# Loading the result rows of an expert layer ahead of a data-dependent loop, and another split of the adds between VectorE and TensorE

## The chip, the cores and the metric

The kernel runs on one core of a Trainium2 chip. The core has five engines, each with an instruction queue of its own: TensorE (PE, matmuls), VectorE (DVE), ScalarE (ACT), GpSimd (POOL) and SyncE (SP, which here only issues transfers); 16 DMA engines move data between the chip's memory (HBM) and the on-chip memory (SBUF). TensorE writes to a small memory of its own, PSUM. The metric is the device time of one execution in microseconds; lower is better.

## What is computed

The reference is one decoder layer on 1024 tokens of width 1024, all in float32: a mixer (gated DeltaNet and dilated attention), a layer norm, a mixture of experts, a second layer norm. The edit lies at the end, in the experts' sum and the second norm. Each token goes to two of 32 experts, and their two results are added, each with its gate:

```python
def grouped_expert_mlp(xf, expert_ids, gates, w_gate, w_up, w_down):
    ...
    def expert_block(args):
        xb, e = args
        hid = jax.nn.silu(xb @ w_gate[e]) * (xb @ w_up[e])
        return hid @ w_down[e]
    ys = lax.map(expert_block, (xs, blk_expert)).reshape(n_slots, d)
    y = jnp.zeros((t + 1, d), F32).at[slot_tok].add(ys.astype(F32) * slot_gate[:, None])
    return y[:t]

# in reference(), at the end of the layer
y = hierarchical_moe(h, w_router_group[l], ...)
x = layer_norm(DEEPNORM_ALPHA * x + (1 + gate2) * y, ln2_g[l], ln2_b[l])
```

## The kernel before, in words

**The experts.** The kernel handles a fixed number of 81 blocks of 32 rows (`SEQ`, `ORDER`), each of one expert. For a block, TensorE transposes the gathered rows (`px`), multiplies them with the expert's gate and up weights (`ph`), and with its down weights (`po`); VectorE scales the result into `yo` (L1378, `block_d`), and GpSimd scatters `yo` by an indirect DMA into `y2d` in HBM (L1329, `scatter_y`), which has one row of 1024 for each token and choice, 2048 rows in all. The weights stand in SBUF in four buffers for gate and up (`wgu0` to `wgu3`, 4 MB each) and three for down (`wd0` to `wd2`, 2 MB each), handed out in turn; `fgu` and `fd` are the lists of free ones. When the last weights are loaded, the next free `wgu` buffer takes the residual stream `x1d` (`xall`, L1486), and the next free `wd` buffer the scale and offset of the norm (`lnb`, L1490).

**The loop for surplus rows.** The fixed blocks hold so many rows for each expert. If more rows come for one, `overflow()` (L1431) handles the surplus in a loop whose count `nov` is read from data on the chip; for the inputs used here the count is zero, and the loop is passed. All engines hold the loop's branch. On either way past it, through the loop or around it, each engine waits until every semaphore that was in use has the value it has at the loop's end; the semaphores named DMAHW belong to transfers that SyncE or ScalarE issued, DMASW to those of GpSimd.

**The final stage.** Two free `wgu` buffers, `yall[0]` and `yall[1]`, take the rows of `y2d`: eight loads on SyncE's queue (L1511), one for each tile of 128 tokens, of 2 x 128 rows of 4 KB. `combine(t)` adds for one tile the two result rows and the residual row, and takes the row sums. It does so in one of three ways, chosen by two tuples of tile numbers: tiles in `DADD` are added on VectorE (L1517), and VectorE adds the residual and sums (L1530, `tensor_tensor_reduce`); tiles in `ASUM` are added on TensorE by matmuls with the identity, all three parts, and ScalarE copies and sums (L1528); for the rest TensorE adds the two result rows, and VectorE adds the residual and sums. Then ScalarE takes the sum of squares (L1533). `norm(t)` computes the reciprocal root with a power function on GpSimd (`rsqrt`, L448), applies scale and offset in two VectorE passes (L1540, L1541), and SyncE stores the tile (L1542). The tiles are written one behind the other, `combine(t)` ahead of `norm(t - 1)`; a scheduler sets the order in each engine's queue from that.

Of the kernel before, what the change touches and what calls it, by code (L numbers as in the profile page):

```python
# [20 lines left out]
P = 128  # L21
D = 1024
S = 1024
NT = S // P
# [99 lines left out]
def build(nc, tc, I, out):  # L124
    V, A, G, T, SY = nc.vector, nc.scalar, nc.gpsimd, nc.tensor, nc.sync

    def mm(o, l, r, start=True, stop=True):
        return T.matmul(o, l, r, start=start, stop=stop)  # L128
# [3 lines left out]
    with es:  # L132
# [17 lines left out]
        y2d = nc.dram_tensor("y2d", [2 * S, D], F32)[:, :]  # L150
# [1170 lines left out]
        def gather_x(pool, idx):  # L1321
            xg = pool.tile([P, 256], F32, name="xg", bufs=XB)
            G.indirect_dma_start(out=xg, out_offset=None, in_=h2v,  # L1323
                                 in_offset=bass.IndirectOffsetOnAxis(ap=idx, axis=0),
                                 bounds_check=4 * S - 1, oob_is_err=False)
            return xg
# [15 lines left out]
        def block_x(pool, psp, xg):  # L1342
            px = psp.tile([P, 2, P], F32, name="px", bufs=2)
            for hh in range(2):
                pe(T.transpose(px[:, hh, :], xg[:, hh * P:(hh + 1) * P], ident))  # L1345
            xT = pool.tile([P, 2, P], F32, name="xT", bufs=3)
            A.copy(xT, px)  # L1347
            return xT

        def block_gu(pool, psp, xT, wgu):  # L1350
            wgu = wgu.rearrange("p (k c x) -> p k c x", k=KD, c=4)
            ph = psp.tile([P, 2, P], F32, name="ph", bufs=2)
            for k in range(KD):
                q, hh = divmod(k, 2)
                for c_ in range(4):
                    pe(mm(ph[32 * c_:32 * c_ + 32], xT[:, hh, 32 * q:32 * q + 32], wgu[:, k, c_],
                          start=(k == 0), stop=(k == KD - 1)))
            th = pool.tile([P, P], F32, name="th", bufs=2)
            A.activation(th, ph[:, 0], AF.Silu)  # L1359
            V.tensor_tensor(th, th, ph[:, 1], op=OP.mult)  # L1360
            return th

        def block_h(pool, psp, th):
            pt = psp.tile([P, P], F32, name="pt", bufs=2)
            pe(T.transpose(pt, th, ident))  # L1365
            hT = pool.tile([P, P], F32, name="hT", bufs=2)
            V.tensor_copy(hT, pt)  # L1367
            return hT

        def block_d(pool, psp, hT, gcol, wd, b_, idx):  # L1370
            wd = wd.rearrange("p (c d) -> p c d", c=4)
            po = psp.tile([P, 256], F32, name="po", bufs=2)
            for c_ in range(4):
                for n_ in range(4):
                    pe(mm(po[32 * n_:32 * n_ + 32], hT[:, 32 * c_:32 * c_ + 32], wd[:, c_, n_ * 256:(n_ + 1) * 256],
                          start=(c_ == 0), stop=(c_ == 3)))
            yo = pool.tile([P, 256], F32, name="yo", bufs=YB)
            V.scalar_tensor_tensor(yo, po, gcol, g2t, op0=OP.mult, op1=OP.mult)  # L1378
            scatter_y(b_, idx, yo)
# [14 lines left out]
        fgu, fd = list(range(NA, 4)), list(range(NA, 3))  # L1394
# [9 lines left out]
        def ring(slot):  # L1404
            return wpools["wgu%d" % slot].tile([P, 2 * KD * FF], F32, name="wgu%d" % slot)

        def ring_d(slot):
            return wpools["wd%d" % slot].tile([P, 4 * D], F32, name="wd%d" % slot)
# [8 lines left out]
        def bx(n):  # L1417
            if n < nb:
                xTs[n] = block_x(xp_, pm_, xgs.pop(n))

        def down(n):
            i, b_ = blocks[n]
            block_d(xp_, pm_, hTs.pop(n), gat[:, b_:b_ + 1], wts[i][1], b_, sct[:, b_:b_ + 1])
            if last[i] == n:
                fd.append(slots[i][1])
# [5 lines left out]
        def overflow():  # L1431
            chain[0] = None
            with tc.For_i(0, nov, 1):
                bh = xp_.tile([P, N2], F32, name="bh", bufs=1)
                V.tensor_scalar(bh, bf_[:, 0], ctr, None, op0=OP.is_equal)
                pc_ = pm_.tile([P, 2], F32, name="px", bufs=2)
                for i in range(2):
                    for q in range(4):
                        for a_ in range(N2):
                            mm(pc_[32 * q:32 * q + 32, i:i + 1], Th[:, i, a_, :], bh[:, a_:a_ + 1],  # L1440
                               start=(a_ == 0), stop=(a_ == N2 - 1))
                ic = xp_.tile([P, 4], I32, name="ic", bufs=1)
                gcl = xp_.tile([P, 4], F32, name="gcl", bufs=1)
                V.tensor_scalar(ic[:, 0:1], pc_[:, 0:1], K["pcol"][:, 1:2], None, op0=OP.add)
                V.tensor_scalar(ic[:, 1:2], ic[:, 0:1], ~(4 * S), None, op0=OP.bitwise_and)
                V.tensor_copy(gcl[:, 0:1], pc_[:, 1:2])
                V.tensor_scalar(gcl[:, 1:2], ctr, float(-NB), None, op0=OP.add)
                el = xp_.tile([P, NE], F32, name="el", bufs=1)
                V.tensor_scalar(el, oend, gcl[:, 1:2], None, op0=OP.is_le)
                V.tensor_reduce(gcl[:, 2:3], el, AX.X, OP.add)  # L1450
                V.scalar_tensor_tensor(ic[:, 2:3], gcl[:, 2:3], 128.0, K["pcol"][:, 0:1], op0=OP.mult, op1=OP.add)
                wgu, wd = ring(fgu[0]), ring_d(fd[0])
                for w_, v_ in ((wgu, wgv), (wd, wdv)):
                    G.indirect_dma_start(out=w_, out_offset=None, in_=v_,
                                         in_offset=bass.IndirectOffsetOnAxis(ap=ic[:, 2:3], axis=0))
                xT = block_x(xp_, pm_, gather_x(xp_, ic[:, 1:2]))
                block_d(xp_, pm_, block_h(xp_, pm_, block_gu(xp_, pm_, xT, wgu)), gcl[:, 0:1], wd, NB, ic[:, 0:1])
                chain[0] = None
                V.tensor_scalar(ctr, ctr, 1.0, None, op0=OP.add)

        ctr = rtk.tile([P, 1], F32, name="ctr")
        V.memset(ctr, float(NB))
# [10 lines left out]
        for n, (i, b_) in enumerate(blocks):  # L1473
# [23 lines left out]
            hTs[n] = block_h(xp_, pm_, th)  # L1497
            bx(n + 2)
        down(nb - 1)
        overflow()  # L1500
        xes.close()

# [1 line left out]
        fps = ExitStack()  # L1504
        fp = fps.enter_context(tc.tile_pool(name="fp", bufs=1, reuse_waits="tile"))
        pf_ = fps.enter_context(tc.tile_pool(name="pf_", bufs=1, space=PSUM))
        yall = [ring(fgu[j]).rearrange("p (t k d) -> p t k d", t=4, k=2) for j in range(2)]
        DADD, ASUM = (0, 4), (1, 3, 5, 7)
        y2r = y2d.rearrange("(k t p) d -> t p k d", k=2, p=P)
        for t in range(NT):  # L1510
            SY.dma_start(yall[t // 4][:, t % 4], y2r[t])  # L1511

        def combine(t):
            ya, yb = (yall[t // 4][:, t % 4, k] for k in range(2))
# [84 lines left out]
```

## Time and profile before

| what | us |
|---|---|
| median of 3 runs (1355.63 to 1357.18) | 1357.07 |
| the profiled execution's own time | 1359.02 |
| its span, first to last instruction | 1357.2 |
| TensorE busy (89% of the span) | 1201.2 |
| VectorE busy (45%) | 616.0 |
| ScalarE busy (25%) | 335.1 |
| GpSimd busy (30%) | 409.3 |

The rows further down come from this one profiled execution. Times are microseconds from the start of the span. A row of the timeline is the start, the duration, the engine, the source line, the operation with its tiles, how many such followed each other, and in brackets how long the engine was idle ahead of it and what ended that. DVE is VectorE, and names that end in q are an engine's sequencer: what it does there (issuing transfers, waiting on semaphores, branching) is no busy time. An idle engine costs nothing where another one, or a transfer, sets the end.

### The profile page before, as it was taken

To read this page: it belongs to the slowest core of one execution; us is meant where nothing else is said; L and a number is where in the kernel's file an instruction comes from. 1 tells how busy PE (TensorE), PEld (TensorE's weight loads), DVE (VectorE), ACT (ScalarE), POOL (GpSimd) and SP (SyncE) were. 2 spreads that over 40 slices of the span, in tenths; PEclk is the share of its full clock that TensorE was granted. 3 is DMA by queue.
4 is the path that set the end of the run, shared out by engine and by line. 5 is a ranking of instruction groups with operands and counts; after the bars stand their busy time and mean duration, and the time that the engine had idled before them with its cause. 6 is when DMAs were issued, how large, how long until landed. Compare 5 with 4: busy or idle time off the path is not lost.

```text
span 1357.2 us, 32321 instructions
## 1 busy us (share of the span) xinstructions
PE 1201.2 (89%) x13901; PEld 813.3 (60%) x13901; DVE 616.0 (45%) x1404; ACT 335.1 (25%) x757; POOL 409.3 (30%) x396
## 2 busy tenths in 40 slices
PE   4898999999997989999988459999699999999956
PEld 0476777868785766867766335555355555555522
DVE  0859385674626747577987731111011111111126
ACT  1654343333322333344211101011011111111003
POOL 0223242332223404131532433333233333333113
PEclk8899999999998989999988659999899999999978
DMA  9210001110114335344436859999999999999965
GB/s 378 98 32 33 33 32 34 47 34 17 48 48 134 129 120 162 121 173 110 138 120 250 354 206 420 425 424 423 428 424 411 374 424 422 424 421 423 409 250 220
DMA packets 50629, 311.13 MB, mean 229 GB/s; under 512 B 10226, under 2 KB 18148, under 8 KB 40756
## 3 DMA queue, kind: packets, MB, share of 16 engines
q1 hardware_dynamic: 36064, 282.60, 52.1%
q0 software_dynamic: 8928, 21.00, 4.1%
q10 hardware_dynamic: 5492, 5.44, 1.2%
q8 instruction: 111, 1.82, 0.5%
q14 instruction: 34, 0.28, 0.1%
HBM read 286.56 MB, written 26.89 MB: 231 GB/s over the span
## 4 chain that ended last, share of the span: by engine, by line
PE 40%; DMA 11%; DVE 10%; issue 4%; POOL 3%; ACT 1%; POOLq 0%; SPq 0%; ACTq 0%; DVEq 0%
PE ph L128 17%; PE po L128 9%; DMA wd<-in_k_wd 8%; PE pj L128 5%; DMA araw<-in_w_ada 2%; PE pc L128 2%; PE pg L128 2%; PE pt L1365 1%; DVE acc L259 1%; PE px L1345 1%; POOL wlo L243 1%; DVE oh L1020 1%; DMA y2d<-yo,sct 1%; PE pg L787 1%; ACT sq L1533 1%
## 5 line engine op out<-in xcount | busy, mean ns | idle before, releaser
L128 PE MATMUL ph<-wgu,xT 128*32 128x256 f32 x5184 | 299.0, 383 | 0.0
L128 PEld LDWEIGHTS ph<-wgu,xT 128*32 128x32 f32 x5184 | 160.3, 110 | 113.7 <-issue 16.3
L128 PE MATMUL pj<-hhi,whi 128*128 128x512 f32 x448 | 193.5, 432 | 5.7 <-ACT akq L500 2.4
L128 PE MATMUL pj<-hlo,whi 128*128 128x512 f32 x448 | 181.5, 405 | 3.1 <-DVE hlo L234 2.9
L128 PE MATMUL pj<-hhi,wlo 128*128 128x512 f32 x448 | 180.9, 404 | 0.0
L128 PE MATMUL po<-wd,hT 128*32 128x256 f32 x2592 | 159.1, 387 | 18.0 <-DMA wd<-in_k_wd 17.5
L1323 POOL DMA_INDIRECT xg<-h2d,idxt x81 | 82.6, 1020 | 273.2 <-PE px L1345 265.9
L1360 DVE TENSOR_TENSOR th<-th,ph 128x128 f32<-128x128 f32 x81 | 23.3, 288 | 303.2 <-ACT th L1359 303.2
L243 POOL TENSOR_TENSOR wlo<-wraw,whi 128x256 fp32r<-128x256 f32 x112 | 96.4, 891 | 205.0 <-ACT whi L240 158.5
L128 PEld LDWEIGHTS po<-wd,hT 128*32 128x32 f32 x2592 | 85.5, 112 | 76.6 <-issue 21.2
L1329 POOL DMA_INDIRECT y2d<-yo,sct x81 | 82.0, 1012 | 67.8 <-DVE hT L1367 42.0
L128 PEld LDWEIGHTS pj<-hhi,whi 128*128 128x128 f32 x448 | 85.5, 191 | 23.1 <-ACT akq L500 2.8
L128 PEld LDWEIGHTS pj<-hlo,whi 128*128 128x128 f32 x448 | 85.7, 191 | 20.0 <-DVE hlo L234 7.6
L128 PEld LDWEIGHTS pj<-hhi,wlo 128*128 128x128 f32 x448 | 85.4, 191 | 17.2 <-issue 0.9
L1378 DVE SCALAR_TENSOR_TENSOR yo<-po,gat,g2t 128x256 f32<-128x256 f32 x81 | 39.2, 484 | 115.2 <-PE po L128 115.2
L1359 ACT ACTIVATE th<-ph 128x128 f32<-128x128 f32 x81 | 22.5, 278 | 262.2 <-PE ph L128 262.2
L1347 ACT COPY xT<-px 128x256 f32<-128x256 f32 x81 | 30.2, 373 | 205.0 <-PE px L1345 205.0
L128 PE MATMUL pg<-akq 128*128 128x512 f32 (+3 forms) x96 | 40.7, 539 | 10.2 <-DVE sm L772 6.1
L128 PE MATMUL pj<-wohi,mhi 128*128 128x512 f32 x112 | 46.8, 418 | 0.0
L128 PE MATMUL pj<-wo,mhi 128*128 128x512 f32 x112 | 45.7, 408 | 0.0
L128 PE MATMUL pc<-vtk,PT 128*128 128x128 f32 x288 | 39.2, 281 | 6.6 <-ACT PT L789 6.4
L128 PE MATMUL pj<-wohi,mlo 128*128 128x512 f32 x112 | 45.0, 402 | 0.0
(698 smaller groups left out, 1784.0 us busy)
## 6 DMA issues: line engine op xcount, KB each, us to landing
wgu<-in_k_wgu SPq DMA_DIRECT2D x32, 4096.0 KB, 16.7
wd<-in_k_wd SPq DMA_DIRECT2D x32, 2048.0 KB, 23.7
araw<-in_w_ada SPq DMA_DIRECT2D x32, 512.0 KB, 4.0
wraw<-in_k_win SPq DMA_DIRECT2D x28, 512.0 KB, 3.5
wad<-in_w_ada SPq DMA_DIRECT2D x8, 1024.0 KB, 10.3
wgu<-y2d SPq DMA_DIRECT2D x8, 1024.0 KB, 11.1
xT<-in_k_xt SPq DMA_DIRECT2D x4, 1024.0 KB, 18.4
xr<-in_x SPq DMA_DIRECT2D x8, 512.0 KB, 4.8
```

Of the source, the lines that this page charges most:

```text
L128: return T.matmul(o, l, r, start=start, stop=stop)
L243: G.tensor_tensor(lo[:, k:k + 2], raw[:, k:k + 2], hi[:, k:k + 2].bitcast(F32), op=OP.subtract)
L259: V.scalar_tensor_tensor(state["acc"], raw, sc[:, k:k + 1], state["acc"], op0=OP.mult, op1=OP.add)
L787: T.transpose(p[:, b_ - b0, :], sc_[:, b_ * P:(b_ + 1) * P], ident)
L1020: V.tensor_scalar(o_, e_, f_, None, op0=OP.is_equal)
L1323: G.indirect_dma_start(out=xg, out_offset=None, in_=h2v, in_offset=bass.IndirectOffsetOnAxis(ap=idx, axis=0), bounds_check=4 * S - 1, oob_ ...
L1329: G.indirect_dma_start(out=y2v[b_], out_offset=bass.IndirectOffsetOnAxis(ap=idx, axis=0), in_=yo, in_offset=None, bounds_check=8 * S - 1, ...
L1345: pe(T.transpose(px[:, hh, :], xg[:, hh * P:(hh + 1) * P], ident))
L1347: A.copy(xT, px)
L1359: A.activation(th, ph[:, 0], AF.Silu)
L1360: V.tensor_tensor(th, th, ph[:, 1], op=OP.mult)
L1378: V.scalar_tensor_tensor(yo, po, gcol, g2t, op0=OP.mult, op1=OP.mult)
```

## The change

The loads of the result rows move from behind the loop to ahead of it, as `load_rows()`. Since the loop's surplus rows are scattered into the same `y2d`, the loop repeats the loads at the end of each of its rounds. The buffers `yall` are taken before the loop, so the loop's own weights go to another buffer (`fgu[2]`). The tuple `DADD` holds five tiles, and `ASUM` three: VectorE adds the rows of tiles 0, 2, 4, 6 and 7, TensorE those of 1, 3 and 5, and no tile is left to the third way.

```diff
@@ overflow(), inside the loop
-                wgu, wd = ring(fgu[0]), ring_d(fd[0])
+                wgu, wd = ring(fgu[2]), ring_d(fd[0])
...
                 V.tensor_scalar(ctr, ctr, 1.0, None, op0=OP.add)
+                load_rows()
@@ behind the last block
         down(nb - 1)
+        yall = [ring(fgu[j]).rearrange("p (t k d) -> p t k d", t=4, k=2) for j in range(2)]
+        y2r = y2d.rearrange("(k t p) d -> t p k d", k=2, p=P)
+
+        def load_rows():
+            for t in range(NT):
+                SY.dma_start(yall[t // 4][:, t % 4], y2r[t])
+
+        load_rows()
         overflow()
         xes.close()
...
-        yall = [ring(fgu[j]).rearrange("p (t k d) -> p t k d", t=4, k=2) for j in range(2)]
-        DADD, ASUM = (0, 4), (1, 3, 5, 7)
-        y2r = y2d.rearrange("(k t p) d -> t p k d", k=2, p=P)
-        for t in range(NT):
-            SY.dma_start(yall[t // 4][:, t % 4], y2r[t])
+        DADD, ASUM = (0, 2, 4, 6, 7), (1, 3, 5)
```

The built programs show what becomes of the order. L1433 is the loop. In each engine's queue the first L1433 branches stand ahead of the loop's body (the second one is the way around it), and the last one, behind the body, ends either way past the loop.

SyncE, from the load of the residual to the loop's branch and, behind the "...", from the end of the loop to the row loads, **before** (wgu_13347 is `xall`, wd_13545 `lnb`, wgu_13869 and wgu_13870 the two halves of `yall`):

```order
L1486 DMA wgu_13347<-x1d 128x8x1024 [waits DMAHW2_49]
L1433 COMPARE_AND_BRANCH
L1433 UNCONDITIONAL_BRANCH
...
L1490 DMA wd_13545<-in_ln_g 128x1024
L1490 DMA wd_13545<-in_ln_b 128x1024
L1511 DMA wgu_13869<-y2d 128x2x1024 [waits DMASW5_49]
L1511 DMA wgu_13869<-y2d 128x2x1024 x3
L1511 DMA wgu_13870<-y2d 128x2x1024 x2
```

SyncE at the same place **now** (wgu_13632 and wgu_13633 are the halves of `yall`):

```order
L1487 DMA wgu_13347<-x1d 128x8x1024 [waits DMAHW2_49]
L1491 DMA wd_13545<-in_ln_g 128x1024 [waits PE_49]
L1491 DMA wd_13545<-in_ln_b 128x1024
L1506 DMA wgu_13632<-y2d 128x2x1024 [waits DMASW5_49,DMASW4_49,DMASW6_49,DMASW3_49,DMASW7_49,DMASW2_49,DMAHW4_49,DMASW1_49,DMASW0_49]
L1506 DMA wgu_13632<-y2d 128x2x1024
L1506 DMA wgu_13632<-y2d 128x2x1024 [waits DMAHW6_49]
...
L1506 DMA wgu_13633<-y2d 128x2x1024 [waits DMAHW3_49]
L1433 COMPARE_AND_BRANCH
L1433 UNCONDITIONAL_BRANCH [waits DMAHW0_49,DMAHW1_49,DMAHW2_49,DMAHW3_49,DMAHW4_49,DMAHW5_49,DMAHW6_49,DMAHW7_49]
```

The norm's weights and all eight row loads stand ahead of the loop, the first row load waits for GpSimd's scatters, and the way around the loop waits for the eight DMAHW semaphores, on which the eight loads count.

GpSimd from the second to last scatter of the fixed blocks to the way around the loop, and then the end of the loop with what follows, **before**:

```order
L1329 DMA y2d<-yo,sct 8192x256 [waits DMASW0_49,DVE_49]
L1381 TENSOR_LOAD novi [waits DMAHW0_49,DMAHW1_49,DVE_49,DMAHW5_49,Activation_49,Pool_49]
L1433 COMPARE_AND_BRANCH
L1433 ISA [waits DMASW3_49,DMASW4_49,DMASW2_49,DMASW1_49]
L1433 UNCONDITIONAL_BRANCH
...
L1329 DMA y2d<-yo,sct 8192x256
```

and **now**:

```order
L1329 DMA y2d<-yo,sct 8192x256 [waits DMASW0_49,DVE_49]
L1329 DMA y2d<-yo,sct 8192x256 [waits DMASW1_49,DVE_49]
L1381 TENSOR_LOAD novi [waits DMAHW0_49,DMAHW1_49,DVE_49,DMAHW5_49,Activation_49,Pool_49]
L1433 COMPARE_AND_BRANCH
L1433 ISA [waits DMASW4_49,DMASW5_49,DMASW3_49,DMASW2_49]
L1433 UNCONDITIONAL_BRANCH
```

The last scatter of the fixed blocks stood behind the loop and stands ahead of it now.

VectorE at the end of the loop and in the first part of the final stage, **before**:

```order
L1433 UNCONDITIONAL_BRANCH [waits DMASW5_49,DMASW4_49,DMASW6_49,DMASW3_49,DMASW7_49,DMASW2_49,DMAHW0_49,DMASW1_49,DMAHW1_49,DMASW0_49,DMAHW2_49,SP_sequencer_49,DMAHW3_49,DVE_sequencer_49,DMAHW4_49,PE_sequencer_49,DMAHW5_49,Activation_s
L1517 TENSOR_TENSOR wgu_13869<-wgu_13869 128x1024 [waits DMAHW4_49]
L1530 ISA wgu_13347,mv<-wgu_13869,wgu_13347 128x1024 [waits DVE_49]
L1530 ISA mv 128x1
L1531 TENSOR_SCALAR mv<-mv 128x1 [waits DVE_49]
L1538 TENSOR_SCALAR mv<-mv 128x1 [waits Activation_49]
L1540 SCALAR_TENSOR_TENSOR wgu_13347<-wgu_13347,mv,wd_13545 128x1024 [waits DMAHW2_49,DVE_49]
L1541 SCALAR_TENSOR_TENSOR wgu_13347<-wgu_13347,mv,wd_13545 128x1024 [waits DMAHW3_49,DVE_49,Pool_49]
```

and **now**:

```order
L1433 UNCONDITIONAL_BRANCH [waits DMASW5_49,DMASW4_49,DMASW6_49,DMASW3_49,DMASW7_49,DMASW2_49,DMAHW0_49,DMASW1_49,DMAHW1_49,DMASW0_49,DMAHW2_49,SP_sequencer_49,DMAHW3_49,DVE_sequencer_49,DMAHW4_49,PE_sequencer_49,DMAHW5_49,Activation_s
L1522 TENSOR_TENSOR wgu_13632<-wgu_13632 128x1024 x2
L1535 ISA wgu_13347,mv<-wgu_13632,wgu_13347 128x1024 [waits DVE_49]
L1535 ISA mv 128x1
L1522 TENSOR_TENSOR wgu_13633<-wgu_13633 128x1024
L1536 TENSOR_SCALAR mv<-mv 128x1 [waits DVE_49]
L1522 TENSOR_TENSOR wgu_13633<-wgu_13633 128x1024 x2
L1543 TENSOR_SCALAR mv<-mv 128x1 [waits Activation_49]
L1545 SCALAR_TENSOR_TENSOR wgu_13347<-wgu_13347,mv,wd_13545 128x1024 [waits DVE_49]
L1535 ISA wgu_13347,mv<-wgu_13632,wgu_13347 128x1024
```

All five adds stand among VectorE's first eight instructions behind the loop, and neither they nor the first passes over `lnb` wait for a transfer of their own; the loop's end does, for the DMASW and DMAHW semaphores alike.

## Rows read from the trace of the kernel before

**Rows 1.** The page's head, and shares of the chain that ended last.

```profile
span 1357.2 us, 32321 instructions
PE 40%; DMA 11%; DVE 10%; issue 4%; POOL 3%; ACT 1%; POOLq 0%; SPq 0%; ACTq 0%; DVEq 0%
```

**Rows 2.** The chain of waits from 1290 on: start, us, what.

```profile
1298.78 3.18 DMA y2d<-yo,sct
...
1303.54 5.78 DMA y2d<-yo,sct
...
1309.76 6.99 DMA wgu<-y2d
```

**Rows 3.** Timeline of the last blocks and the start of the final stage.

```profile
1290.46 1.91 PE L128 MATMUL po<-wd,hT 128*32 128x256 f32 x32
...
1298.02 0.48 DVE L1378 SCALAR_TENSOR_TENSOR yo<-po,gat,g2t 128x256 f32<-128x256 f32 x1 [1.13 <-PE po L128]
...
1298.78 0.98 POOL L1329 DMA_INDIRECT y2d<-yo,sct  x1 [4.60 <-DVE hT L1367]
...
1300.76 0.48 DVE L1378 SCALAR_TENSOR_TENSOR yo<-po,gat,g2t 128x256 f32<-128x256 f32 x1 [2.06 <-PE po L128]
1303.02 0.35 SPq L1490 DMA_DIRECT2D wd<-in_ln_g  x1
...
1309.34 6.67 SPq L1511 DMA_DIRECT2D wgu<-y2d  x8
1314.20 1.23 DVE L1517 TENSOR_TENSOR wgu<-wgu 128x1024 f32<-128x1024 f32 x1 [12.96 <-DMA wgu<-y2d]
...
1316.79 3.56 PE L128 MATMUL ps<-wgu,kc 128*128 128x512 f32 x4 [8.79 <-DMA wgu<-y2d]
```

**Rows 4.** The loop's line L1433 and its body's first line L1435 (duration ns min/median/max).

```profile
L1433 SPq EVENT_SEMAPHORE  x12: 27/28/13000, 1288.1 to 1302.8; - x12
L1433 DVEq EVENT_SEMAPHORE  x13: 21/50/50, 1301.8 to 1303.2; - x13
L1433 PEldq COMPARE_BRANCH  x3: 97/197/3388, 1300.2 to 1305.7; - x3
nothing on L1435; most used: ['L128', 'L1345', 'L787', 'L1329', 'L1323', 'L536', 'L1347', 'L1365', 'L1359', 'L1378', 'L243', 'L1140', 'L988', 'L993', 'L772', 'L998', 'L798', 'L1360', 'L1367', 'L1433', 'L470', 'L777', 'L811', 'L568', 'L708']
```

**Rows 5.** Stretch, us; PE, PEld, DVE, ACT, POOL busy; granted clock, DMA share, GB/s.

```profile
1314.20:1328.00 13.80, 11.21 (x23) 5.01 (x24) 7.84 (x13) 3.60 (x6) 3.09 (x2) 0.79 1.03 413
1328.00:1343.37 15.37, 15.37 (x38) 6.76 (x37) 15.03 (x24) 7.20 (x12) 5.83 (x4) 1.00 0.65 258
1314.20:1352.42 38.22, 28.45 (x62) 12.34 (x62) 28.37 (x42) 14.39 (x24) 11.85 (x8) 0.86 0.70 281
1303.00:1320.00 17.00, 5.29 (x6) 2.01 (x7) 3.98 (x6) 1.24 (x2) 2.54 (x2) 0.50 0.75 287
1320.00:1344.00 24.00, 24.00 (x57) 10.64 (x56) 19.04 (x29) 9.94 (x17) 7.37 (x5) 1.00 0.76 302
```

**Rows 6.** Groups of instructions between 1314.2 and 1352.42: busy us, mean ns, idle before.

```profile
L1541 DVE SCALAR_TENSOR_TENSOR wgu<-wgu,mv,wd 128x1024 f32<-128x1024 f32 x8 | 10.2, 1281 | 1.3 <-POOL mv L448 1.3
L1528 ACT ACTIVATE wgu<-ps 128x1024 f32<-128x1024 f32 x4 | 4.1, 1024 | 7.2 <-PE ps L128 7.2
L1530 DVE CUSTOM_DVE_ANT_0 wgu<-wgu,wgu 128x1024 f32<-128x1024 f32 x2 | 2.4, 1223 | 0.0
L1517 DVE TENSOR_TENSOR wgu<-wgu 128x1024 f32<-128x1024 f32 x2 | 2.4, 1220 | 13.0 <-DMA wgu<-y2d 13.0
L1530 DVE DVE_READ_ACCUMULATOR2_ANT mv<- 128x1 f32 x4 | 0.3, 84 | 0.0
```

**Rows 7.** Timeline of the final stage: one power function, and the last VectorE operation.

```profile
1330.72 1.27 DVE L1540 SCALAR_TENSOR_TENSOR wgu<-wgu,mv,wd 128x1024 f32<-128x1024 f32 x1
1330.88 1.52 POOL L448 TENSOR_TENSOR mv<-mv,pio 128x1 f32<-128x1 f32 x1 [3.54 <-DVE mv L1538]
...
1351.14 1.28 DVE L1541 SCALAR_TENSOR_TENSOR wgu<-wgu,mv,wd 128x1024 f32<-128x1024 f32 x1 [0.44 <-POOL mv L448]
```

## The prediction

> **What bounds the kernel now.** I read the page first: the span is 1357.2 us, and of the chain of work that ended last 40% is TensorE, most of it the expert matmuls before the edit [rows 1]. The edit touches nothing before the last experts, so the stage to read is the last 57 us, and there the chain of waits and the timeline. The chain leaves compute at 1298.78 for a scatter of result rows that takes 3.18 us to land, then for another of 5.78 us, then for 6.99 us of row loads [rows 2]. The timeline gives the engines. VectorE ends the last block's result at 1300.76 + 0.48 = 1301.24; the last scatter leaves GpSimd only at 1303.54 [rows 2], because it stands behind the branch of the overflow loop; SyncE issues the eight row loads from 1309.34, when that scatter has landed; VectorE begins the final stage at 1314.20 after 12.96 us of idleness, TensorE at 1316.79 after 8.79 us [rows 3]. The loop does nothing: no instruction of its body's first line stands in the trace [rows 4]. Passing it still costs each engine a row of waits on semaphores, 12 or 13 records of the loop's line [rows 4].
>
> From 1314.20 the loads bound the stage, then VectorE. The DMA engines run at 1.03 of their share and 413 GB/s up to 1328.00, and VectorE is busy for only 7.84 of those 13.80 us; from 1328.00 to 1343.37 it is busy for 15.03 of 15.37 [rows 5]. So before the change about 14 us of loading lie beside work of the final stage. That overlap is what the change can lose.
>
> **The change, part by part.** The order says where the loads go: on SyncE ahead of the loop's branch, and the row behind them, the way past the loop, waits for all eight queues on which they run. VectorE's way past the loop waits for the DMA queues too, and its adds have no wait of their own any more. So I take it that no tile is touched before the eighth load has landed. The steps, from the unchanged 1301.24:
>
> *The last scatter* now stands ahead of the branch. The one before it began 0.28 us behind its VectorE operation (1298.02 + 0.48 to 1298.78) [rows 3], so it begins at 1301.52 and not at 1303.54. Its landing is 3.18 or 5.78 us [rows 2]. The long one ran beside the loads of the norm's weights, issued at 1303.02. These wait in the changed order for TensorE alone, for the down matmuls of the third block from the end, over at 1290.46 + 1.91 = 1292.37 [rows 3]; they should be nearly through by 1301.5. I take 3.18: landed at 1304.70 (bound 1307.3).
>
> *The eight row loads* start there and not at 1309.34: 4.64 us gained. The first tile was there at 1314.20, 4.86 us after the first issue, the second at 1316.79 [rows 3]. At 413 GB/s [rows 5] a load of 2 x 128 x 1024 floats (1.049 MB) takes 2.54 us, which agrees with the 2.59 us between the two. The eighth is then there 4.86 + 7 x 2.56 = 22.8 us after the first issue, at 1327.5. SyncE issues nothing else there that could be late.
>
> The Trainium skill (DMA: Bandwidth & Descriptors, Specifications) puts the limit of the memory for one core at about 358 GB/s, below what the loads reach here; by that figure 8.39 MB would need 23.4 us and not 20.3, and the time would be some 3 us more. The rows show 413 GB/s over 13.8 us, and the measurement decides.
>
> *The way past the loop* costs from the eighth landing to VectorE's first add. VectorE's 12 waits there lie between 1301.8 and 1303.2 [rows 4], about 0.1 us each; five of them stand behind the one on the eighth load, and SyncE must first pass its own on. I take 1.0 us: VectorE begins at 1328.5 and not at 1314.20, **14.3 us later**. The bounds are 0.3 us and the 3.4 us that TensorE's sequencer spent on one branch there (3388 ns) [rows 4], if VectorE meets the like; TensorE's own is hidden under the wait for the loads.
>
> *VectorE's work.* From 1314.20 to 1352.42 it was busy for 28.37 us of 38.22 in 42 instructions [rows 5]. The edit gives it three more adds of 1.22 us, and one more sum-with-statistics (tile 7, that ScalarE did) of 1.22 with its read of 0.08 [rows 6]: 28.37 + 3.66 + 1.30 = 33.3 us. TensorE loses 14 of 32 matmuls (each two passes) and ScalarE one pass over a tile; neither was the bound late in the stage, so that is worth nothing here.
>
> *VectorE's idleness* of 9.85 us was waiting for loads and, at the end, for a single tile's chain. With all rows in place and three adds early in its row, VectorE has work until the end. What stays are short waits for GpSimd's power function: 1.3 us over three tiles before [rows 6]. I take the busy share of the saturated stretch, 15.03 / 15.37 = 0.978 [rows 5]: 33.3 / 0.978 = 34.1 us. Bounds: 33.3, and 36.8 if each of eight tiles waits 0.44 us (a third of 1.3). VectorE ends at 1328.5 + 34.1 = 1362.6.
>
> *The end.* The last VectorE operation ended at 1351.14 + 1.28 = 1352.42 [rows 7], 4.78 us ahead of the span's end: storing the last tile. Unchanged: 1362.6 + 4.8 = 1367.4.
>
> **The sum**: later start 14.3, more VectorE work 5.0, less idleness 9.85 - 0.75 = 9.1: **+10.2 us** on the span of 1357.2. The profiled execution took 1359.02, 1.95 above the median of the three runs shown; I put the difference on the median: 1357.07 + 10.2 = **1367.3 us**, 0.75% slower.
>
> **The rivals.**
> *Early loads, early work.* If the engines are not held at the loop (each tile is used when it lands), the 4.64 us of earlier loading are a gain: 1357.07 - 4.6 = 1352.4, faster by 0.34%. For it: it is what the chain shows, 5.78 and 6.99 us of DMA ahead of all compute [rows 2]. Against it: the order's waits, and the trace, where each engine has its row of semaphore records at the loop's line although the loop does nothing [rows 4].
> *TensorE at half clock.* It idles from the last block (over by 1300.76 [rows 3]) to about 1328.6. After the shorter pause before, the granted clock was 0.50 of full speed (1.2 GHz) up to 1320, and 1.00 (2.4 GHz) from there [rows 5], with a first stretch of four passes in 3.56 us, 0.89 each [rows 3]; at 1.00 it was 24.00 / 57 = 0.42 [rows 5]. The changed kernel's 36 passes take 4 x 0.89 + 32 x 0.42 = 17 us if the clock comes back as it did, out of VectorE's way. Should it stay low, they take 36 x 0.89 = 32 us from 1328.6: tile 5's sum is there at 1360.6, ScalarE's pass over it (1.02 us) [rows 6] ends at 1361.7, and in the changed order 11.8 us of VectorE's row stand behind that (eight wide passes of 1.28, one sum of 1.22 and small ones): 1373.5 + 4.8, which is 1378. Against it: the matmuls come in one unbroken row, as from 1316.79 on.
> *GpSimd shut out by VectorE.* GpSimd's power function for a tile began at 1330.88 beside a wide VectorE operation (1330.72 to 1331.99) and ended at 1332.40, 0.41 us after it [rows 7]. If it can end only after a wide operation, and VectorE now runs one behind another, each tile's last step waits: the upper bound above, 36.8 for 34.1, 1370.0. The Trainium skill (SBUF — State Buffer, Who interferes with whom) states that a VectorE instruction with two SBUF inputs and a GpSimd instruction that reads SBUF shut each other out for a whole instruction; the rows fit that.
> *Not what it says.* If the loads stood behind the loop after all, five adds would lie under the loads, where VectorE idles 6 of 13.8 us [rows 5]: no change, 1357. The order speaks against it.
>
> **How the numbers follow.** About 0.2% is what a measurement of this kernel can tell from no change. Forecast 0.75, GpSimd shut out 0.12, half clock 0.05: slower, 0.92. Early work, faster: 0.05. Not what it says, the same: 0.03. The range takes the forecast with its bounds. Upward these are the scatter +2.6, the branch +2.4 and the waits for GpSimd +2.7, of which I let two come together and some of the third: 1373. Downward they are the idleness -0.8, the way past the loop -0.7 and the loads -2.5, if all 8.39 MB came at 413 GB/s from the first issue on, 20.3 us for 22.8: 1363. It holds the forecast and the third rival, and leaves out the rest.
>
> **What would show it.** Right: the last scatter at about 1301.5, the first row load at about 1304.7, the eighth landed at about 1327.5, VectorE's first add after that and about 27 us behind its last operation on the blocks, then hardly a gap in VectorE until about 1362.6. Wrong: an add on VectorE before the eighth load is in (then faster); idle stretches of VectorE over 1 us that TensorE or ScalarE end (half clock); a gap ahead of each tile's last step that GpSimd ends (the third rival); or a start long after the landing, a branch as long as TensorE's.

## The result, and the profile after

The changed kernel takes 1365.74 us (median of four runs, 1365.27 to 1370.3), the kernel before beside it 1357.09: a ratio of 1.008, with a 95% interval of 1.006 to 1.010. The forecast was 1367.3, in a range of 1363 to 1373, slower. The kernel is 8.65 us slower, where 10.2 were predicted. The sign, the place and the mechanism held; several terms had the wrong size, and the reasons given for two terms were wrong, as the experiments and the trace show. Three single executions among the experiments below, of 1546 to 3161 us, were disturbed ones and are in no ratio; the profile of e6 fell on one of them, so its row of the table has no stage.

The profiled execution is the longest of the four; its own time is 1370.3 us, and its span stands in the page's head, which answers to [rows 1]:

```profile
span 1368.5 us, 32268 instructions
```

In it everything ahead of the final stage runs some 2 us later than in the profile before: VectorE's last operation on the blocks ends at 1302.75 + 0.48 = 1303.23, there at 1301.24. So all stages are measured here from that point, **the end of the blocks**, to the end of the span. Before, that was 1357.2 - 1301.24 = 56.0 us; now it is 1368.5 - 1303.23 = 65.3 us, 9.3 more.

The timeline of the changed kernel, which answers to [rows 3] (start, duration, engine, line, operation, count, and in brackets the idle time ahead with what ended it; the adds are now on L1522, the row loads on L1506):

```profile
1302.75 0.48 DVE L1378 SCALAR_TENSOR_TENSOR yo<-po,gat,g2t 128x256 f32<-128x256 f32 x1 [2.06 <-PE po L128]
1303.51 0.98 POOL L1329 DMA_INDIRECT y2d<-yo,sct  x1 [1.76 <-DVE yo L1378]
1306.26 8.01 SPq L1506 DMA_DIRECT2D wgu<-y2d  x8
1331.26 2.36 DVE L1522 TENSOR_TENSOR wgu<-wgu 128x1024 f32<-128x1024 f32 x2 [28.03 <-SPq L1433]
...
1331.36 5.15 PE L128 MATMUL ps<-wgu,kc 128*128 128x512 f32 x6 [28.68 <-SPq L1433]
```

The scatter and the loads are early, as the change means them to be, 0.28 and 3.03 us after the end of the blocks (2.30 and 8.10 before). But VectorE and TensorE stand idle for 28 us, and what releases both is not a load: it is SyncE's sequencer on L1433, the loop's line. Before, VectorE idled for 12.96 us and was released by a load [rows 3]. The records of that line, which answer to [rows 4] (durations in ns, then first and last start):

```profile
L1433 SPq EVENT_SEMAPHORE  x20: 17/28/28, 1322.8 to 1332.0; - x20
L1433 DVEq EVENT_SEMAPHORE  x13: 21/50/50, 1303.8 to 1331.0; - x13
L1433 PEldq COMPARE_BRANCH  x3: 97/193/3547, 1302.2 to 1331.1; - x3
```

The first of VectorE's 13 semaphore records began at 1303.8 and the last at 1331.0: the same count as before, when all lay between 1301.8 and 1303.2 [rows 4]. The loop's body is still not run, and it still holds every engine until the loads in front of it have landed. The stretches of the stage show it from the other side (stretch, its length, busy time with count of PE, PEld, DVE, ACT and POOL, granted clock, DMA share, GB/s):

```profile
1312.00:1318.00 6.00, 0.00 (x0) 0.00 (x0) 0.00 (x0) 0.00 (x0) 0.00 (x0) 0.50 1.02 416
1318.00:1324.00 6.00, 0.00 (x0) 0.00 (x0) 0.00 (x0) 0.00 (x0) 0.00 (x0) 0.50 1.02 410
...
1332.00:1340.00 8.00, 8.00 (x15) 3.38 (x14) 8.00 (x11) 2.12 (x3) 1.61 (x1) 0.75 0.00 0
1340.00:1350.00 10.00, 9.39 (x22) 3.80 (x20) 9.56 (x17) 5.08 (x10) 5.14 (x4) 1.00 0.39 157
...
1331.26:1364.37 33.11, 18.02 (x36) 7.68 (x36) 31.96 (x47) 13.16 (x22) 11.96 (x8) 0.76 0.25 100
```

Read this against [rows 5]: before, VectorE worked 7.84 us of the 13.80 in which the loads filled the DMA engines. Now the loads run at the same rate, 410 to 416 GB/s, and no engine works beside them; then the engines work, and no load runs. After the hold VectorE is busy for 31.96 of 33.11 us, where it was busy for 28.37 of 38.22.

### The profile page after: what moved, and what is told of

Read it like the earlier page. It is cut to its first block, busy times and chain, and to the rows that moved or that the text cites. A ratio compares the mean times of both kernels' runs of the same rounds, so it can differ in the third digit from the quotient of the medians.

```text
span 1368.5 us, 32268 instructions
## 1 busy us (share of the span) xinstructions
PE 1189.6 (87%) x13873; PEld 809.2 (59%) x13873; DVE 618.8 (45%) x1409; ACT 333.8 (24%) x755; POOL 409.8 (30%) x396
## 5 line engine op out<-in xcount | busy, mean ns | idle before, releaser
L128 PE MATMUL pg<-akq 128*128 128x512 f32 (+3 forms) x96 | 39.9, 530 | 10.2 <-DVE sm L772 6.0
L448 POOL TENSOR_TENSOR mv<-mv,pio 128x1 f32<-128x1 f32 x16 | 16.5, 1032 | 97.0 <-DVE mv L1119 49.1
## 6 DMA issues: line engine op xcount, KB each, us to landing
wad<-in_w_ada SPq DMA_DIRECT2D x8, 1024.0 KB, 10.5
```

Of the source, the lines that this page charges most:

```text
L448: G.tensor_tensor(o, x, e.to_broadcast(list(x.shape)), op=OP.pow)
```

## The experiments

Each group of four kernels ran on one chip, with the kernel before beside them, and each ratio is against that one. The **stage** is the time from the end of the blocks to the end of the span, in the one profiled execution of each kernel.

| kernel | ratio, 95% interval | first add after the end of the blocks | VectorE from its first add to its end | stage |
|---|---|---|---|---|
| before | 1 | 12.96 | 38.2 | 56.0 |
| changed | 1.008 (1.006 to 1.010) | 28.03 | 33.1 | 65.3 |
| e1, loads ahead, old split | 1.0104 (1.0082 to 1.0126) | 27.90 | 37.8 | 70.5 |
| e2, new split alone | 0.999 (0.9969 to 1.001) | 11.65 | 38.8 | 54.2 |
| e3, changed, no loop | 0.9966 (0.9945 to 0.9988) | 7.83 | 37.5 | 49.5 |
| e4, before, no loop | 0.9968 (0.995 to 0.9986) | 7.78 | 38.1 | 50.7 |
| e5, four loads ahead | 1.0001 (0.9984 to 1.0018) | 16.89 | 36.0 | 57.7 |
| e6, one load ahead | 0.997 (0.9948 to 0.9991) | | | |
| e9, e6 again | 0.9994 (0.9974 to 1.0015) | 9.67 | 38.8 | 53.3 |
| e7, changed, even split | 1.0053 (1.0036 to 1.007) | 28.37 | 32.0 | 64.5 |
| e8, scatter ahead, loads behind | 0.9982 (0.9963 to 1.0002) | 9.23 | 38.0 | 52.1 |
| e10, one load ahead, even split | 0.9948 (0.9928 to 0.9968) | 10.01 | 36.3 | 51.2 |
| e11, changed again | 1.007 (1.0043 to 1.0097) | 27.91 | 33.1 | 65.2 |
| e12, e8 with even split | 0.9964 (0.9944 to 0.9985) | 9.29 | 36.2 | 50.3 |

### One part of the change at a time (e1, e2)

e1 is the changed kernel with the old tuples:

```diff
-        DADD, ASUM = (0, 2, 4, 6, 7), (1, 3, 5)
+        DADD, ASUM = (0, 4), (1, 3, 5, 7)
```

> The change's loads ahead of the loop with the old split of the adds (VectorE tiles 0 and 4, TensorE 1, 3, 5, 7, and 2 and 6 shared). Theory (the hold: every engine waits at the loop until the eighth load is in): first add about 28 us after VectorE's last operation on the blocks, as in the changed kernel; then TensorE's 64 passes set the end, 4 at 0.89 and 60 at about 0.44 us, 30 us, and 7.2 us from its last pass to VectorE's last operation as before the change: about 1370 us, some 5 us slower than the changed kernel. Rival (the five adds on VectorE are what costs, the place of the loads is not): 1352 to 1357 us.

e2 is the kernel before with the new tuples, the same two lines the other way round, loads behind the loop.

> The loads behind the loop as before, with the change's split of the adds (five tiles on VectorE, three on TensorE). Theory (the hold): not slower than before; VectorE starts at about 1314 when tile 0 lands, has 33 us of work and some 2 us of waits for later tiles, ends at 1349 to 1351 instead of 1352.4: 1353 to 1356 us. Rival (VectorE's added work is the cost): 5 to 9 us slower than before, 1362 to 1366 us.

Moving the loads alone costs 1.0% and 14.5 us of stage. The new split alone costs nothing: 0.999, where the theory had it a little faster and the rival slower by up to 0.7%; the rival is excluded, the theory's gain of up to 4 us is at most half there (1.8 us of stage, of which 1.3 are that the loads of that execution were issued earlier, 6.80 us after the end of the blocks and not 8.10). So the loss is the moved loads. What VectorE waits for in e1, beside the hold, says what the new split is good for (engine and line that waited, for whom, us in total, times, longest):

```profile
DVE mv L1543 <- ACT sq L1538: 6.6, 5, 1.4
DVE mv L1536 <- ACT wgu L1533: 1.4, 1, 1.4
DVE wgu L1546 <- POOL mv L448: 1.4, 3, 0.5
```

In the changed kernel only the last of the three is left, beside the hold itself:

```profile
DVE wgu L1522 <- SPq L1433: 28.0, 1, 28.0
...
DVE wgu L1546 <- POOL mv L448: 1.1, 3, 0.4
```

With the old split VectorE waits six times for ScalarE, 8.0 us in all: five times for the sum of squares of the tile at hand (L1538), with no other tile's work between in its queue, and once for a tile that ScalarE sums when TensorE has added it (L1533). TensorE's 64 passes run in one unbroken row of 30 us, against 18 us for the 36 of the changed kernel. The two runs differ in the split alone; how much of the waiting is TensorE's pace, and how much the order in VectorE's queue, no run separates.

```profile
1328.41 30.43 PE L128 MATMUL ps<-wgu,kc 128*128 128x512 f32 x64 [28.64 <-SPq L1433]
```

### The loop taken out (e3, e4)

Both leave out the call of `overflow()`, so surplus rows would not be handled; there are none in these inputs. e3 is the changed kernel without it, e4 the kernel before.

```diff
         load_rows()
-        overflow()
         xes.close()
```

> The changed kernel without the loop for surplus rows (that part of the computation is left out; there are no surplus rows in these inputs). Theory (the hold): the row loads start about 3 us after the last block as in the changed kernel, but each tile is used when it lands; VectorE's first add about 8 to 9 us after its last operation on the blocks and not 28; it is then busy for 33 us with 1 to 3 us of waits: 1347 to 1352 us, some 15 us faster than the changed kernel. Rival (VectorE's added work): within 3 us of the changed kernel, 1362 to 1366 us.

> The kernel before without the loop for surplus rows (left out as in the run above), old split. It prices what the loop costs the kernel before: its last scatter and the norm's weights wait behind the loop there. Theory: the row loads start about 4.6 us earlier, and the end follows them: 1352 to 1353 us. If the loop is free where the loads stand behind it: 1356 to 1358 us.

e3 is the run that decides. With no loop to pass, the same early loads feed the engines as they land: VectorE's first add is released by a load, 7.83 us after the end of the blocks, 5.21 us after the first load's issue, and the stage is 15.8 us shorter than the changed kernel's (e3). On the time of the kernel before, 1357.09, its ratio makes 1352.5 us, at the edge of what the theory had; VectorE then still idled for 4.8 us, where 1 to 3 were expected:

```profile
1305.07 6.86 SPq L1506 DMA_DIRECT2D wgu<-y2d  x8
1310.28 1.23 DVE L1521 TENSOR_TENSOR wgu<-wgu 128x1024 f32<-128x1024 f32 x1 [7.83 <-DMA wgu<-y2d]
```

The loads' early place was never the fault; the hold at the loop was. e4 shows that the loop costs the kernel before some 5 us too (stage 50.7 for 56.0, ratio 0.9968, as expected): the scatter behind the branch, and the loads behind that. Against e4 the whole change is worth 1.2 us of stage in e3, and nothing that the two ratios tell apart.

### How long the hold is (e5, e6, e9)

e5 puts four of the eight loads ahead of the loop and four behind it, e6 one and seven; e9 is e6 a second time, and its profiled execution is the one read here.

```diff
-                load_rows()
+                load_rows(range(4))
...
-        def load_rows():
-            for t in range(NT):
+        def load_rows(ts):
+            for t in ts:
...
-        load_rows()
+        load_rows(range(4))
         overflow()
+        load_rows(range(4, NT))
```

> The changed kernel, but only the loads of tiles 0 to 3 stand ahead of the loop; those of tiles 4 to 7 stand behind it. Theory (no engine passes the loop until every load ahead of it has landed): the hold ends with the fourth landing and not with the eighth. In the changed kernel the fourth landed 16.5 us after VectorE's last operation on the blocks and the first add came 0.8 us after the last landing, so VectorE starts 17 to 18 us after the blocks (28.0 in the changed kernel); the other four loads are issued there, are all in 13 us later, while VectorE has work for 16 us on the first four tiles. VectorE needs 33 to 34 us from its start and the end 4.2: the stage takes 55 to 57 us against 65.3 of the changed kernel, some 9 us less; against the kernel before the time is 0.998 to 1.004. Rival (the changed kernel is slow for another reason than the landing of what stands ahead of the loop, such as the place of the loads on the queue or the adds): the stage stays at 63 us or more, ratio 1.006 or more.

> The changed kernel with the load of tile 0 alone ahead of the loop, the other seven behind it. Theory: the hold ends with one landing. The first load landed 9.3 us after VectorE's last operation on the blocks in the changed kernel (it shared the queues with seven more) and some 4.4 us after its issue in the kernels without the loop, so VectorE starts 8 to 10.5 us after the blocks; the other loads follow there, tile 1 is in 5 us later, and the rest at 2.6 us each, so VectorE waits for tiles until about 28 us after the blocks. The stage takes 50 to 54 us, a ratio of 0.996 to 1.000 against the kernel before. With the runs that hoist four and eight the start should be a straight line: 2.6 us for each load that stands ahead of the loop. Rival (a fixed price for loads that are issued ahead of the loop): a start of 15 us or more whatever their number.

> The kernel with one load ahead of the loop, a second time, since the first look at it was at an execution that the chip disturbed. Theory: the hold ends with the one landing. VectorE starts 9 to 10 us after its last operation on the blocks (28.0 with eight loads ahead, 16.9 with four); the stage takes 50 to 53 us, ratio 0.995 to 0.999 against the kernel before. Rival (a fixed price): a start of 15 us or more.

VectorE's first adds, of e5, and of e9:

```profile
1306.51 15.40 SPq L1506 DMA_DIRECT2D wgu<-y2d  x8
1319.97 2.36 DVE L1523 TENSOR_TENSOR wgu<-wgu 128x1024 f32<-128x1024 f32 x2 [16.89 <-DMA wgu<-y2d]
```

```profile
1308.55 11.13 SPq L1506 DMA_DIRECT2D wgu<-y2d  x8
1315.33 1.23 DVE L1523 TENSOR_TENSOR wgu<-wgu 128x1024 f32<-128x1024 f32 x1 [9.67 <-DMA wgu<-y2d]
```

The hold grows with the loads ahead of the loop: 9.67, 16.89 and 28.03 us for one, four and eight, (28.03 - 9.67) / 7 = 2.6 us for each, which is a load at 410 GB/s. The start of e9 alone could be the plain wait for its first tile; that of e5 can't, since the last packet of tile 0 came at 1311.4 and VectorE began on it at 1319.97. There is no fixed price: the rival of 15 us or more falls. e5 comes out even with the kernel before (1.0001), as expected, though its stage of 57.7 lies just above the 55 to 57, and its first add just ahead of the 17 to 18. One load ahead gives the 8 to 10.5 us expected, and a ratio that two measurements put at 0.997 and 0.9994, the second just above what was expected of it, as is the stage: VectorE then waits again for rows and first chains, 38.8 us for 33.1.

### Another split under the hold (e7, e11)

```diff
-        DADD, ASUM = (0, 2, 4, 6, 7), (1, 3, 5)
+        DADD, ASUM = (0, 2, 4, 6), (1, 3, 5, 7)
```

> The changed kernel, but TensorE adds tile 7's rows again: VectorE adds four tiles (0, 2, 4, 6), TensorE four (1, 3, 5, 7). It takes an add of 1.22 us and a sum with its read (1.30 us) from VectorE, and gives TensorE 12 more passes. Theory (under the hold all rows are there at the start, and VectorE's busy time sets the length): VectorE works 30.6 to 31.2 us where it worked 33.1, and the kernel is some 2 to 2.5 us faster than the changed kernel: stage 62.8 to 63.5, ratio against the kernel before 1.003 to 1.007 where the changed kernel has 1.008 (1.006 to 1.010). Rival (TensorE, half as fast at its start after the hold, sets the end, as it did with the old split): the stage is 65 us or more, no faster than the changed kernel.

> The changed kernel itself on the chip of the other runs, to set it beside the even split under the hold (ratio 1.0053, 1.0036 to 1.0070) and beside the kernels with fewer loads ahead. Expected: ratio 1.006 to 1.010, stage 65 to 66 us, VectorE's first add 28 us after the blocks. If the even split is worth its 2.5 us of VectorE's work, this kernel comes out at 1.007 or more; if TensorE sets the end there, at 1.005.

The even split under the hold brings the kernel to 1.0053, against 1.008 and 1.007 for the changed one: the intervals overlap, so a gain of 0.2% is likely and not certain, and the 1.007 of e11 decides it neither way. In the stage it is 0.8 us (0.7 against e11), not the 2 to 2.5 of the theory, and between theory and rival:

```profile
1328.21:1360.18 31.97, 22.99 (x48) 9.83 (x48) 29.91 (x44) 14.12 (x24) 10.78 (x8) 0.87 0.26 104
```

VectorE's busy time fell as it should, 31.96 to 29.91, but nearly half came back as idleness (1.15 to 2.06), and the hold in that execution was 0.3 us longer. TensorE does not set the end: its 48 passes are over 23 us into the 32.

### The scatter early, the loads behind the loop (e8, e10, e12)

e8 leaves all loads behind the loop, and gives the loop's body a dependence on the last scatter's rows and on the norm's weights, so that those two are issued ahead of it, as in the changed kernel:

```diff
-                block_d(xp_, pm_, block_h(xp_, pm_, block_gu(xp_, pm_, xT, wgu)), gcl[:, 0:1], wd, NB, ic[:, 0:1])
+                block_d(xp_, pm_, block_h(xp_, pm_, block_gu(xp_, pm_, xT, wgu)), gcl[:, 0:1], wd, blocks[-1][1], ic[:, 0:1])
...
-                load_rows()
+                V.tensor_copy(gcl[:, 3:4], lnb[:, 0, 0:1])
...
+        overflow()
         load_rows()
-        overflow()
```

> The new split of the adds with all eight loads behind the loop, but the loop's body is given dependences on the last scatter and on the norm's weights, so that these two are issued ahead of the loop as in the changed kernel. It tells what the earlier scatter is worth without the hold. Theory: the scatter lands 2.7 us after its issue, 3 us after VectorE's last operation on the blocks; the way past the loop costs 0.8 to 1.5 us, so the first load is issued at 4 to 4.5 us (8.1 in the kernel before, 6.8 in the run with the split alone) and the first tile's add begins 4.5 to 5 us later. Everything behind moves ahead by that: VectorE ends at 46.5 to 48, the stage takes 50 to 52.5 us against 56.0 of the kernel before and 54.2 with the split alone, ratio 0.995 to 0.998. Rival (the scatter's landing is only waited for elsewhere, at the loop's end, and the loads move little): stage 54 us or more, ratio 0.998 to 1.001.

e10 is e6 with the even split, e12 is e8 with it.

> One load ahead of the loop, and the adds in even halves: VectorE adds tiles 0, 2, 4 and 6, TensorE tiles 1, 3, 5 and 7. VectorE has one add and one sum less (2.5 us). Theory: without the long hold VectorE waits some 5 us for the first tiles' chains (loads and ScalarE's sums), and its work behind them sets the end, so the 2.5 us come off: stage 48 to 50.5 us, ratio 0.993 to 0.997. Rival (the loads and the chain of the first tiles set VectorE's end, and less work is only more waiting, as with the new split against the old one without the hold): no more than 1 us faster than the kernel with one load ahead and the uneven split.

> All eight loads behind the loop, the last scatter and the norm's weights ahead of it, and the even split of the adds. Theory: as the kernel with the uneven split (stage 52.1 us, VectorE's first add 9.2 us after the blocks) less the 2.5 us of VectorE's work: stage 49.5 to 50.5, ratio 0.994 to 0.998. Rival (the first tiles' chains set the end): stage 51 to 52.

The scatter ahead of the branch brings the first load from 8.10 to 3.91 us after the end of the blocks (4 to 4.5 expected), and the stage to 52.1 us, as expected; the ratio of 0.9982 lies at the edge between theory and rival, and the stage excludes the rival. The even split, worth little under the hold, is worth its price without it: 38.8 to 36.3 us of VectorE from e9 to e10, 38.0 to 36.2 from e8 to e12. The stage of e10, 51.2 us, is 0.7 above the expectation, that of e12 within it. e10 is the fastest of these at 0.9948, e12 at 0.9964 can't be told from it; both beat both kernels of this study, and neither holds the engines for more than one load.

```profile
1314.59:1350.92 36.33, 23.13 (x48) 9.36 (x48) 30.69 (x44) 14.06 (x24) 10.79 (x8) 0.88 0.77 303
```

This is e10 from its first add: loads (DMA share 0.77) and work lie beside each other again.

## Why the prediction was right, and where it was not

Times from the end of the blocks, predicted (from 1301.24) and measured (from 1303.23):

| step | predicted | measured |
|---|---|---|
| last scatter on GpSimd | 0.28 | 0.28 |
| first row load | 3.46 | 3.03 |
| VectorE's first add | 27.3 | 28.03 |
| VectorE's end | 61.4 | 61.1 |
| end of the span | 66.2 | 65.3 |

**The hold** is the step on which the sign hung, and it was shown by taking it away (e3) and by its length (e5, e9). The later start was put at 14.3 us and measured 28.03 - 12.96 = 15.1.

**The scatter's landing** was taken as 3.18 us and was 2.75 (1303.51 to 1306.26). The 5.78 us of [rows 2], kept as a bound, did not come back: the norm's weights, issued at 1294.43, were all but through (the last packets of their queue ended at 1304.1).

**The eight loads and the way past the loop** were put at 22.8 + 1.0 us and measured 1331.26 - 1306.26 = 25.0. At 410 to 416 GB/s the rate was as predicted; the end was not. The DMA view of the last microseconds, in 40 slices of 0.1 us:

```profile
GB/s 451 410 369 533 328 410 451 369 410 410 369 410 82 123 41 41 41 0 41 41 0 41 41 0 41 0 41 41 0 0 0 0 0 0 0 0 0 0 0 0
```

It covers 1327 to 1331. At 1328.2, 21.9 us after the first issue, the flow is over, and then single packets come up to 1329.8: one straggling DMA engine with its share. The last packet ended at 1329.93, so the loads took 23.7 us for 22.8, and the way past the loop 1.3 us for 1.0. In the first 6 us of the loads the view of the queues has one entry more in the changed kernel than in e3, which has no loop. The changed kernel:

```profile
q1 hardware_dynamic: 448, 1.77, 79.3%
q8 instruction: 1, 0.02, 1.8%
```

and e3:

```profile
q1 hardware_dynamic: 451, 1.78, 81.1%
```

One packet of instructions, 1.8% of 16 engines over 6 us, which is 1.7 us of one engine. The straggler is there from the first load on. Each load ends with 16 packets of 4 bytes, as many as there are DMA engines; the views count them as under 512 B. Of the first load's, in the changed kernel 15 come up to 1310.80, and one in the next 1.8 us (1309.99 to 1310.80, then to 1312.60):

```profile
DMA packets 94, 0.32 MB, mean 400 GB/s; under 512 B 15, under 2 KB 15, under 8 KB 94
DMA packets 183, 0.75 MB, mean 414 GB/s; under 512 B 1, under 2 KB 1, under 8 KB 183
```

and in e3 all 16 within 0.8 us (1309.00 to 1309.80):

```profile
DMA packets 91, 0.31 MB, mean 384 GB/s; under 512 B 16, under 2 KB 16, under 8 KB 91
```

In the changed kernel the sixteenth came 1.3 us behind the fifteenth, at the first load and still at the eighth. The packets of the other traces agree. The data of the first load begin 1.0 us after its issue. In all six profiles in which a packet of instructions begins 0.9 to 2.0 us after that issue (changed, e1, e7, e9, e10, e11), the sixteenth of the first load comes 0.8 to 1.5 us behind the fifteenth; in the four without one beside the loads' start (before, e2, e3, e4) it comes 0.1 to 0.3 us behind, and in the three where one begins earlier (e5, e8, e12) 0.4 us or less. So the straggler goes with that packet, and the packet with the way past the loop; the lag doesn't follow the packet's length (1.77 us and a lag of 1.3 in the changed kernel, 1.21 and 1.5 in e1). That the packet is code which an engine fetches for its jump is inferred from the queue's name.

**VectorE's added work** is the mis-sized term. It was priced by the instructions' durations, 1.22 us for an add or a sum, 5.0 us in all. But neighbours overlap: where one wide operation follows another, the next begins 1.14 us later, as the chain of the changed kernel has it (start, us, what):

```profile
1333.62 1.14 DVE wgu L1535
1334.77 1.14 DVE wgu L1522
```

From e4 to e3, with the same early loads, the split adds 32.69 - 28.35 = 4.3 us of busy time; with no waits between, in the changed kernel, 31.96 - 28.37 = 3.6.

```profile
1311.09:1349.22 38.13, 28.50 (x62) 12.34 (x62) 28.35 (x42) 14.39 (x24) 11.78 (x8) 0.86 0.69 277
```

```profile
1310.28:1347.73 37.45, 14.84 (x30) 6.23 (x30) 32.69 (x47) 13.06 (x22) 12.99 (x8) 0.68 0.70 283
```

(e4, then e3, each from VectorE's first add to its end.)

**VectorE's idleness** shrank from 9.85 us to 33.11 - 31.96 = 1.15; predicted was 0.75. But the reason given was wrong, so that this term came out near by luck. The prediction put the old idleness down to the loads and took TensorE's relief as worth nothing. The waits of the kernel before, behind its first add, say otherwise: no load, and 8.3 us for ScalarE:

```profile
DVE mv L1538 <- ACT sq L1533: 5.5, 5, 1.4
DVE mv L1531 <- ACT wgu L1528: 2.8, 1, 2.8
DVE wgu L1541 <- POOL mv L448: 1.3, 3, 0.5
```

And e1 has all rows in place and the old split, and VectorE is idle for 37.80 - 28.25 = 9.55 us of it:

```profile
1328.22:1366.02 37.80, 30.43 (x64) 13.10 (x64) 28.25 (x42) 14.39 (x24) 11.84 (x8) 0.86 0.24 98
```

So under the old split the rows in place save 0.3 us. The two rows from e4 and e3 above tell what the split does with loads under way: idle 9.78 with the old one, 4.76 with the new. Only both together let VectorE work through: with the new split the rows in place save another 3.6, from 4.76 to 1.15. A sign of it stood in [rows 6], with 7.2 us of ScalarE's idleness ended by TensorE.

**The end** took 4.16 us and not 4.78, and it isn't the store of the last tile, as the prediction has it. Two rows of GpSimd in the kernel before: its last power function (start, duration in us), and DRAIN, an instruction of its sequencer at the close of the program (durations in ns, min/median/max, then first and last start):

```profile
1349.63 1.47 POOL L448 TENSOR_TENSOR mv<-mv,pio 128x1 f32<-128x1 f32 x1 [2.99 <-DVE mv L1538]
L1595 POOLq DRAIN  x3: 40/109/6827, 1349.6 to 1357.0; - x3
```

and the same two in the changed one:

```profile
1360.93 1.45 POOL L448 TENSOR_TENSOR mv<-mv,pio 128x1 f32<-128x1 f32 x1 [2.21 <-DVE mv L1543]
L1600 POOLq DRAIN  x3: 40/109/6808, 1360.9 to 1368.3; - x3
```

The first DRAIN begins with that power function, takes 6.8 us, and ends at 1356.4 and 1367.7, 0.8 us ahead of the span's end; in the kernel before SyncE had seen the last store in at 1355.4. In 11 of the 13 profiles read here the span ends 7.6 us after the start of the last power function; in e2 and e3, where SyncE's wait for the last store is over later than GpSimd's DRAIN, it ends 7.7 and 8.1 us after it. That start lay 2.79 us ahead of VectorE's end before, and 3.44 now, which is the 0.7.

Sum of the stage: +15.1 later start, +3.6 work, -8.7 idleness, -0.7 end: +9.3 us, against +10.2: the errors of the four terms, +0.8, -1.4, +0.4 and -0.7, cancel in part. The medians differ by 8.65.

**The rivals.** Early loads with early work did not happen in the changed kernel; e3 shows the time it would give. TensorE's clock came back as after the shorter pause: granted 0.50 up to the first pass, 0.75 on the mean from 1332 to 1340, as it rose, and 1.00 behind, 36 passes in 18.02 us for 17. GpSimd was shut out, but at a small price:

```profile
1338.39 2.67 POOL L448 TENSOR_TENSOR mv<-mv,pio 128x1 f32<-128x1 f32 x1 [33.90 <-DVE mv L1543]
...
1339.41 1.22 DVE L1535 CUSTOM_DVE_ANT_0 wgu<-wgu,wgu 128x1024 f32<-128x1024 f32 x1
```

It took 2.67 us beside two wide VectorE operations, 1.52 beside one [rows 7], and ended 0.43 us behind the second of the two, there 0.41 behind the one. The Trainium skill (SBUF — State Buffer, Who interferes with whom) has a VectorE instruction with two SBUF inputs contend with a GpSimd instruction that reads SBUF; the rows agree. VectorE waited for GpSimd only 1.1 us, since it had other tiles' work meanwhile.

## What to carry to other kernels

In a program built like this one, where each engine's way past a data-dependent loop waits for every semaphore in use, work placed ahead of the loop is waited for there by every engine, even if the loop runs zero times: put there only what is done by the time the last engine arrives (here the scatter and one load), and the rest behind. What is released by the last of several transfers is timed by the slowest DMA engine, not by the mean rate (1.3 us later here). And when work is moved from one engine to another, ask who waits for the relieved engine's chain before calling the relief worth nothing; price added operations in a busy row by the distance of their starts. The busiest engine's last operation need not set the end either.

## What was not expected of the hardware

A packet of instructions (0.02 MB) that comes near the start of the loads, as the engines pass the loop, takes 0.9 to 2.1 us in six profiles, and one DMA engine then trails the other 15 by 0.8 to 1.5 us; in the changed kernel it does so to the end of the loads, by 1.3 us. A power function of one element a partition on GpSimd can take 2.67 us, as long as two wide VectorE operations. And GpSimd's closing DRAIN runs for 6.8 us from the start of its last power function, before the change and after; in 11 of 13 profiles it, and no store, set the end.
